# T tiles with 64 bytes more each, and the matrix of ones kept in the first stage's pool

## The chip, the cores and the metric

The kernel runs on one core of one Trainium2 chip. Its time is device time in microseconds (us). Five engines matter: TensorE (PE; its weight loads are PEld), VectorE (DVE), ScalarE (ACT), GpSimd (POOL), and SyncE (SP), which here issues every DMA.

## The reference

One encoder layer is applied to two batches, a prompt of 512 tokens and a sample of 1024, with the same weights and a model width of 1024. After an RMS norm, one input projection gives q, k, v and a gate for each of two attention branches, and two merge gates:

```python
    h = rmsnorm(x, norm_g)
    proj = h @ w_in
    qa, ka, va, za, qb, kb, vb, zb, ga, gb = jnp.split(proj, np.cumsum(SPLITS)[:-1], axis=-1)
    ...
    oa = neighbourhood_attention(qa, ka, va, rpb_a) * jax.nn.silu(za)
    oa = oa @ w_o_a
    ...
    ob = window_gqa_attention(qb, kb, vb, t5_table, sink_b) * jax.nn.silu(zb)
    ob = ob @ w_o_b
    merged = jax.nn.sigmoid(ga) * oa + jax.nn.sigmoid(gb) * ob
    return x + merged @ w_out
```

## The kernel before, in words

**Numbers.** Every float32 operand of a large product is split into two parts of type float32r: a high part (ACT copies it, L1104) and a low part (the source less the high part, DVE or POOL, L1109). A product is then three matmuls for each block of 128 rows, in `product`: high by high (L1221), high by low (L1222), low by high (L1223). The weights `whi`, `wlo` are loaded into the array, and 512 columns (256 in the very last product) of the other operand are moved through it. Sums over four or eight blocks stay in one of the PSUM banks p, s, o, t.

**Stages.** Norm of the prompt; attention of the prompt (projections L725, scores L919, softmax, transposes L968, products with v L1005); dense stage of the prompt (gates z, merge gates, branch projections, output projection); then attention and the dense stage of the sample. In `dense_phase` a pair of output blocks is either classic (eight blocks of h directly) or made with seven products in Strassen's way, for which sums of blocks of h are needed as moving operand. The prompt has only classic pairs (`CLASSIC_P`), the sample has three Strassen pairs of z, eight of the merge gates and three of the output projection (`CLASSIC_S`).

**The tiles called T.** Three kinds of operand share this name. (1) The sums of blocks of h for z and the merge gates of the sample: four sums, high and low, loaded from `t_d` by way of `U` and split in `stored_sums`. (2) The gated branches, split in `split_u`: four tiles for the prompt, in a pool of its own (`u_pool`); eight for the sample. (3) The sums of blocks of the merged activations, made on DVE in the tiles `S` and split in `sums`, ahead of the sample's output projection. A tile has 4 x 512 numbers per partition (8192 bytes), one slice of 512 for each block k. The eight tiles of the sample lie side by side in one pool and are used in turn by all three kinds. So the matmuls that read T are, for the prompt, 8 blocks x 2 branches x 4 k x 3 = 192; for the sample 384 with gated branches and 14 pairs x 4 products x 4 k x 3 = 672 with sums, 1056 in all.

**Where tiles lie.** The constants' pool (`cpool`) ends with a tile `left_pad` that serves only to fill it up; `right_pad` does so at the other end. Counted from the sizes in the order of allocation, T, whi, wlo, raw, S, U, C, the gates' `ot` and the sample's hh and hl all begin at a multiple of 512 bytes of their partition. The attention's tiles do not: pp (the transposed softmax, moving operand of L1005) begins 224 bytes past a multiple, hb (a gathered copy of h for branch B, loaded as weights in L725) 448 past.

**Order.** A planner (`Flow.run`) simulates the engines with fixed costs and writes out each engine's program: an operation starts when its inputs are ready and its tile's turn has come, lowest `prio` first, on the engine of its choice that ends first. It knows the number of buffers of a tile, not their size. DMAs are all issued on SP in the planned order. A tile allocated over older ones waits for their last readers.

**`ones`.** A matrix of 128 x 128 ones, set by DVE at the start (L404), is the stationary operand of a small matmul in `spread_rstd` (L453) that spreads a token's norm factor over the partitions.

Of the kernel before, what the change touches and what calls it, by code (L numbers as in the profile page):

```python
# [10 lines left out]
F32 = mybir.dt.float32  # L11
F32R = mybir.dt.float32r
# [13 lines left out]
CLASSIC_S = (1, 0, 1)  # L26
START = (-10, -6.5, -4, -3)
GATE = 2
FIRST_POOL = (0, 2)
NORM = (-20, -1, 0, 1)  # L30
P = 128
# [312 lines left out]
def encoder_kernel(  # L344
# [24 lines left out]
    dve = nc.vector  # L369
    pe = nc.tensor  # L370
# [29 lines left out]

    mhalf = cpool.tile([P, 8], F32, tag="mhalf", name="mhalf")
    dve.memset(mhalf, -0.5)
    ones = cpool.tile([P, P], F32, tag="ones", name="ones")
    dve.memset(ones, 1.0)  # L404
    gx = cpool.tile([P, KC], F32, tag="gx", name="gx")

    cpool.tile([P, 56], F32, tag="left_pad", name="left_pad")
# [8 lines left out]
    f = Flow(pspool)  # L416
# [27 lines left out]
    def spread_rstd(pool, r, t, rb, prio):  # L444

        diag = f.value(pool, [P, P], F32, "diag", 1)
        f.op(
            (("act", ACT_(P) + 40),), lambda e: act.activation(diag.t, ident, AF.Copy, scale=r.t),
            prio, new=[diag], use=[r],
        )  # L450
        ps = f.value(pspool, [P, 512], F32, "o", 2)
        f.op(
            (("pe", 215),), lambda e: pe.matmul(ps.t[:, :P], ones, diag.t, start=True, stop=True),  # L453
            prio, new=[ps], use=[diag],
        )
        f.op(
            (("act", ACT_(P, False)),),
            lambda e: act.activation(rb.t[:, t * P : (t + 1) * P], ps.t[:, :P], AF.Copy), prio, use=[ps],
            **({"into": [rb]} if t else {"new": [rb]}),
        )  # L460
# [609 lines left out]
    def dense_phase(geo, hh, hl, h_ops, o_stores, exps_done, start, opened, tp, up, p0, p1, p2, x_t, y_t, classic, after_gates=None, side=None):  # L1070
# [3 lines left out]
        nh = 512  # L1074
# [17 lines left out]

        dma = f.dma

        def tt(out, in0, in1, op, n, prio, psum=False, **kw):

            choice = (("dve", DVE_(n)),) if psum else any_tt(n)
            return f.op(choice, lambda e: engines[e].tensor_tensor(out(), in0(), in1(), op=op), prio, **kw)
# [16 lines left out]
        def moving_sums(tv, ops):  # L1115
            def mov(j):
                vh, vl = tv[j]
                return [(lambda k=k: vh.t[:, k], lambda k=k: vl.t[:, k], ops[j, k], [vh, vl]) for k in range(4)]

            return mov  # L1120

        def sums(prio, done):

            tv = [tuple(f.value(tp, [P, 4, sn], F32R, "T", 8) for _ in range(2)) for _ in range(4)]
            ops = {}
            for k in range(4):
                blk = lambda a, kk, n: (lambda: a.t[:, kk, n * sn : (n + 1) * sn].bitcast(F32))
                h = {(i, n, a): blk((hh, hl)[a], k + 4 * i, n) for i in range(2) for n in range(2) for a in range(2)}
                t = [tile_("S", 3) for _ in range(4)]

                def step(j, in0, block, part, op, new, other=None):
                    after = done[k + 4 * block[0], block[1]] if done else []
                    kw = {"new": [t[j]]} if new else {"into": [t[j]]}
                    use = [v for v in (other, None if new else t[j]) if v]
                    tt(
                        lambda v=t[j]: v.t[:, :sn], in0, h[*block, part], op, sn, prio, use=use, after=after, hold=[hh, hl], **kw
                    )


                for j, plus, minus in ((0, (0, 1), (0, 0)), (2, (1, 1), (0, 1))):  # L1140
                    after = done[k + 4 * plus[0], plus[1]] + done[k + 4 * minus[0], minus[1]] if done else []
                    tt(
                        lambda v=t[j]: v.t[:, :sn], h[*plus, 0], h[*minus, 0], ALU.subtract, sn, prio, new=[t[j]], after=after,
                        hold=[hh],
                    )
                    step(j, lambda v=t[j]: v.t[:, :sn], plus, 1, ALU.add, False)
                    step(j, lambda v=t[j]: v.t[:, :sn], minus, 1, ALU.subtract, False)
                after = done[k + 4, 1] if done else []
                tt(
                    lambda v=t[1]: v.t[:, :sn], h[1, 1, 0], lambda v=t[0]: v.t[:, :sn], ALU.subtract, sn, prio,  # L1150
                    new=[t[1]], use=[t[0]], after=after, hold=[hh],
                )
                step(1, lambda v=t[1]: v.t[:, :sn], (1, 1), 1, ALU.add, False)
                step(3, lambda v=t[1]: v.t[:, :sn], (1, 0), 0, ALU.subtract, True, t[1])
                step(3, lambda v=t[3]: v.t[:, :sn], (1, 0), 1, ALU.subtract, False)
                for j in (0, 2, 1, 3):
                    vh, vl = tv[j]
                    ops[j, k] = split(
                        lambda vh=vh, k=k: vh.t[:, k], lambda vl=vl, k=k: vl.t[:, k], lambda v=t[j]: v.t[:, :sn], sn, prio,
                        (vh, k == 0), (vl, k == 0), [t[j]],  # L1160
                    )

            return moving_sums(tv, ops)

        def stored_sums(prio):

            tv, ops = {}, {}
            for j in (1, 2, 0, 3):
                tv[j] = tuple(f.value(tp, [P, 4, nh], F32R, "T", 8) for _ in range(2))
                vh, vl = tv[j]  # L1170
                for k in range(4):
                    st = tile_("U", 4)
                    dma(
                        lambda st=st, j=j, k=k: nc.sync.dma_start(st.t, t_d[j, k]), 512 * nh, prio, new=[st],
                        after=[s[j] for s in t_stores],
                    )
                    ops[j, k] = split(
                        lambda vh=vh, k=k: vh.t[:, k], lambda vl=vl, k=k: vl.t[:, k], lambda st=st: st.t, nh, prio,
                        (vh, k == 0), (vl, k == 0), [st],
                    )  # L1180
            return moving_sums(tv, ops)
# [182 lines left out]
        def split_u(c, a, n, v, prio):  # L1364
            br, k = divmod(c, 4)
            key = br, a // nh
            new = key not in uv
            if new:
                uv[key] = tuple(f.value(up, [P, 4, nh], F32R, "T", 4 * len(halves)) for _ in range(2))
            vh, vl = uv[key]  # L1370
            cols = slice(a % nh, a % nh + n)
            u_ops.setdefault((*key, k), []).extend(split(
                lambda: vh.t[:, k, cols], lambda: vl.t[:, k, cols], lambda: v.t[:, :n], n, prio, (vh, new), (vl, new), [v],
            ))

        def with_x(c, a, n, v, prio):
# [64 lines left out]
        for m in range(8):  # L1441
# [5 lines left out]
            for n in halves:  # L1447
                gs_ = []
                for br in range(2):
                    ps = psum_(next(tags))  # L1450
                    vh, vl = uv[br, n]
                    movs = [
                        (lambda k=k, vh=vh: vh.t[:, k], lambda k=k, vl=vl: vl.t[:, k], u_ops[br, n, k], [vh, vl])
                        for k in range(4)
                    ]
                    product(ps, ws[br], movs, prio, True, True)
                    tag, bufs = (("C", n_c), ("ot", n_ot) if short else ("U", 4))[br]
                    g = tile_(tag, bufs)
                    dma(
                        lambda g=g, br=br, m=m, n=n: nc.sync.dma_start(g.t, g_d[br, m, :, half[n]]), 512 * nh,  # L1460
                        prio - 0.5, new=[g], after=stores["g", br, m, n],
                    )
                    tt(
                        lambda g=g: g.t, lambda ps=ps: ps.t, lambda g=g: g.t, ALU.mult, nh, prio, psum=True,
                        use=[ps, g], into=[g],
                    )
                    gs_.append(g)
                a, b = gs_
                tt(lambda a=a: a.t, lambda a=a: a.t, lambda b=b: b.t, ALU.add, nh, prio, use=gs_, into=[a])
                m_ops[m, n] = split(  # L1470
                    lambda m=m, n=n: hh.t[:, m, half[n]], lambda m=m, n=n: hl.t[:, m, half[n]], lambda a=a: a.t, nh,
                    prio, (hh, None), (hl, None), [a], after=h_reads,
                )
# [37 lines left out]

    f.stage(-1000, open=(r_h, d0["p"], rb_pool, early["p"], late["p"], norm_p), make=h_p)
    f.dma(lambda: nc.sync.dma_start(gx, norm_g), 4096, START[0] + 0.2, into=[gx_v])
    for t in range(gp.nb):
        h_ops["p"][t] = norm_tile(norm_p, x_p, *h_p, t, NORM[t], START[t], h_ops["p"][t - GATE][::2] if t >= GATE else ())
    setup(norm_p, gp.nb)
# [113 lines left out]
```

## Time and profile before

| what | value |
|---|---|
| median of three runs | 1195.18 us (1193.61 to 1196.21) |
| the profiled execution's own time | 1193.63 us |
| its span, first to last instruction | 1191.8 us |
| mean granted TensorE clock | 0.996 |
| PE, DVE, ACT, POOL busy, share of the span | 97%, 74%, 55%, 29% |
| HBM traffic | 137 GB/s over the span |

The span is that of one execution, and its times of day below count from its first instruction. A matmul's duration includes its passage through the array, and its end is modelled; the pace of a run of matmuls is read from starts. An engine's idle time is put down to what ended it.

### The profile page before, as it was taken

The page shows a single profiled execution, that of the slowest core. Times are in us where ns is not written, and L with a number is a line of the kernel's source. Part 1 is how long each engine was busy: PE and PEld are TensorE (multiplying, and loading weights), DVE is VectorE, ACT ScalarE, POOL GpSimd, SP SyncE. Part 2 cuts the span into 40 slices and gives each one's busy share as a digit, 9 for nine tenths or more (in the row PEclk, how much of TensorE's full clock was granted, in tenths as well). Part 3 has the DMA queues.
Part 4 walks back from the last instruction along what each step waited for, and adds up shares of the span by engine and source line. Part 5 has one row for each costly group of instructions (what it writes and reads, how often), then busy time and mean ns, then how long its engine had stood idle before and what let it go on. Part 6 is the DMA issues. An engine that isn't in the chain of part 4 may idle for free.

```text
span 1191.8 us, 18682 instructions
## 1 busy us (share of the span) xinstructions
PE 1156.6 (97%) x6118; PEld 981.4 (82%) x6118; DVE 878.8 (74%) x1977; ACT 660.0 (55%) x1504; POOL 342.5 (29%) x469
## 2 busy tenths in 40 slices
PE   7999899999999999999999989999999999999798
PEld 6889777888888898998997878878888888788687
DVE  6788888586655468878777888868976565497985
ACT  6967886453433346465669888866434344333330
POOL 4763654000011043343326454302311110131110
PEclk9999999999999999999999999999999999999999
DMA  9734223778875422120211122237773334573152
GB/s 302 258 110 137 80 65 106 215 237 259 261 212 180 152 74 63 26 66 22 78 50 50 34 63 45 45 103 265 198 220 133 104 118 156 191 246 107 46 176 97
DMA packets 124545, 159.35 MB, mean 134 GB/s; under 512 B 28272, under 2 KB 66928, under 8 KB 124448
## 3 DMA queue, kind: packets, MB, share of 16 engines
q1 hardware_dynamic: 124448, 158.16, 43.7%
q8 instruction: 48, 0.79, 0.3%
q14 instruction: 49, 0.40, 0.1%
HBM read 121.40 MB, written 41.44 MB: 137 GB/s over the span
## 4 chain that ended last, share of the span: by engine, by line
PE 83%; DVE 5%; POOL 3%; ACT 2%; issue 2%; DMA 1%; ACTq 0%; POOLq 0%; DVEq 0%
PE p L725 20%; PE s L919 5%; PE p L1221 5%; PE p L1223 5%; PE p L1222 4%; PE o L1005 4%; PE s L1221 4%; PE s L1222 4%; PE s L1223 4%; PE t L968 4%; PE o L1223 4%; PE o L1222 4%; PE o L1221 4%; PE t L1222 4%; PE t L1223 4%; PE t L1221 4%
## 5 line engine op out<-in xcount | busy, mean ns | idle before, releaser
L1104 ACT ACTIVATE whi<-raw 128x512 fp32r<-128x512 f32 (+1 forms) x160 | 92.5, 589 | 79.2 <-PE s L1222 18.0
L1109 POOL TENSOR_TENSOR wlo<-raw,whi 128x512 fp32r<-128x512 f32 (+1 forms) x34 | 46.3, 1361 | 310.7 <-ACT whi L1104 298.1
L725 PE MATMUL p<-wlo,hh 128*128 128x384 f32 x384 | 133.7, 348 | 0.0
L725 PE MATMUL p<-whi,hh 128*128 128x384 f32 x384 | 133.7, 348 | 0.0
L725 PE MATMUL p<-whi,hl 128*128 128x384 f32 x384 | 132.8, 346 | 0.0
L895 ACT ACTIVATE sb<-sb,mx 128x384 f32<-128x384 f32 (+1 forms) x192 | 108.9, 570 | 20.2 <-DVE mx L886 19.3
L1109 DVE TENSOR_TENSOR wlo<-raw,whi 128x512 fp32r<-128x512 f32 (+1 forms) x126 | 82.1, 662 | 38.9 <-ACT whi L1104 38.8
L725 PE MATMUL p<-whi,hb 128*128 128x384 f32 x384 | 108.8, 351 | 1.3 <-DVE qk L630 1.0
L979 DVE TENSOR_TENSOR pp<-t,pp 128x512 fp32r<-128x512 f32 (+1 forms) x136 | 84.8, 640 | 27.8 <-ACT pp L974 26.2
L974 ACT ACTIVATE pp<-t 128x512 fp32r<-128x512 f32 (+1 forms) x136 | 73.0, 558 | 46.2 <-PE t L968 45.8
L1005 PE MATMUL o<-pp,v 128*128 128x256 f32 (+1 forms) x368 | 81.9, 333 | 3.9 <-DVE pp L979 3.9
L950 POOL TENSOR_TENSOR sb<-sb,rs 128x384 f32<-128x384 f32 (+1 forms) x95 | 71.5, 770 | 45.6 <-DVE rs L944 40.1
L968 PE MATMUL t<-ident,sb 128*128 128x128 f32 x496 | 75.8, 277 | 7.4 <-DVE pp L979 4.9
L760 POOL TENSOR_TENSOR rs_r<-rs_v,mhalf 128x4 f32<-128x4 f32 (+1 forms) x72 | 80.3, 1115 | 5.4
L725 PEld LDWEIGHTS p<-whi,hh 128*128 128x128 f32 x384 | 72.6, 189 | 3.6 <-issue 2.9
L725 PEld LDWEIGHTS p<-whi,hb 128*128 128x128 f32 x384 | 69.7, 191 | 6.5 <-issue 2.2
L968 PEld LDWEIGHTS t<-ident,sb 128*128 128x128 f32 x496 | 57.9, 140 | 20.5 <-DVE pp L979 7.1
L725 PEld LDWEIGHTS p<-whi,hl 128*128 128x128 f32 x384 | 72.6, 189 | 1.9 <-issue 1.0
L725 PEld LDWEIGHTS p<-wlo,hh 128*128 128x128 f32 x384 | 72.6, 189 | 1.4 <-issue 1.0
L753 POOL TENSOR_SCALAR rs_v<-ss 128x4 f32<-128x4 f32 (+1 forms) x72 | 17.3, 241 | 183.2 <-DVE ss L746 178.7
L1005 PEld LDWEIGHTS o<-pp,v 128*128 128x128 f32 x368 | 58.2, 189 | 11.0 <-DVE pp L979 7.4
L725 PE MATMUL p<-wlo,hb 128*128 128x384 f32 x192 | 67.1, 350 | 0.0
(348 smaller groups left out, 3227.0 us busy)
## 6 DMA issues: line engine op xcount, KB each, us to landing
raw<-in_w_g_dram SPq DMA_DIRECT2D x96, 256.0 KB
w<-in_w_att_dram SPq DMA_DIRECT2D x48, 384.0 KB
g_d<-C SPq DMA_DIRECT2D x48, 256.0 KB
ot<-o_d SPq DMA_DIRECT2D x36, 256.0 KB
raw<-in_w_z_dram SPq DMA_DIRECT2D x32, 256.0 KB
raw<-in_w_out_dram SPq DMA_DIRECT2D x32, 256.0 KB
C<-g_d SPq DMA_DIRECT2D x24, 256.0 KB
out_dram<-C SPq DMA_DIRECT2D x23, 256.0 KB
```

The source lines that it names most:

```text
L725: pe.matmul(ps.t[:, :GW], part[u](k), mv.t[:, c], start=k == 0 and m == 0, stop=k == KC - 1 and m == 2,)
L760: lambda e: nc.gpsimd.tensor_tensor(r.t[:, :nn], rv.t[:, :nn], mhalf[:, :nn], op=ALU.pow),
L895: act.activation(sb.t[:, :width], sb.t[:, :width], AF.Exp, bias=mx.t[:, i : i + 1], scale=-1.0, accum_out=sm.t[:, i : i + 1],)
L968: pe.transpose(pt.t[:, u * P : (u + 1) * P], sbs[i].t[:, c * P : (c + 1) * P], ident)
L974: lambda e, pt=pt, pp=pp, nn=nn: act.activation(pp.t[:, 0, :nn], pt.t[:, :nn], AF.Copy),
L979: lambda e, pt=pt, pp=pp, nn=nn: dve.tensor_tensor(pp.t[:, 1, :nn], pt.t[:, :nn], pp.t[:, 0, :nn].bitcast(F32), op=ALU.subtract),
L1005: pe.matmul(out(), v.t[:, vs], mv(), start=first, stop=last)
L1104: (("act", ACT_(n)),), lambda e: act.activation(hi(), src(), AF.Copy), prio,
L1109: lambda e: engines[e].tensor_tensor(lo(), src(), hi().bitcast(F32), op=ALU.subtract), prio,
L1221: pe.matmul(out, hi.t[:, cs], mh(), start=first and k == 0, stop=False)
L1222: pe.matmul(out, hi.t[:, cs], ml(), start=False, stop=False)
L1223: pe.matmul(out, lo.t[:, cs], mh(), start=False, stop=last and k == len(ws) - 1)
```

## The change

Each T tile gets 16 numbers (64 bytes) more per partition, and is allocated as a flat row, of which `part(v, k, n)` cuts slice k. The eight tiles of the sample together take 512 bytes more. These come from `ones`, which leaves the constants' pool: it becomes a tile of the first norm stage's pool, set by an operation of the planner with the lowest `prio` of that stage.

```diff
+T_PAD = 16
...
-    ones = cpool.tile([P, P], F32, tag="ones", name="ones")
-    dve.memset(ones, 1.0)
...
-            (("pe", 215),), lambda e: pe.matmul(ps.t[:, :P], ones, diag.t, start=True, stop=True),
-            prio, new=[ps], use=[diag],
+            (("pe", 215),), lambda e: pe.matmul(ps.t[:, :P], ones.t, diag.t, start=True, stop=True),
+            prio, new=[ps], use=[diag, ones],
...
+        def part(v, k, n):
+
+            return v.t[:, k * n : k * n + n]
...
-                return [(lambda k=k: vh.t[:, k], lambda k=k: vl.t[:, k], ops[j, k], [vh, vl]) for k in range(4)]
+                return [(lambda k=k: part(vh, k, sn), lambda k=k: part(vl, k, sn), ops[j, k], [vh, vl]) for k in range(4)]
...
-            tv = [tuple(f.value(tp, [P, 4, sn], F32R, "T", 8) for _ in range(2)) for _ in range(4)]
+            tv = [tuple(f.value(tp, [P, 4 * sn + T_PAD], F32R, "T", 8) for _ in range(2)) for _ in range(4)]
...
-                tv[j] = tuple(f.value(tp, [P, 4, nh], F32R, "T", 8) for _ in range(2))
+                tv[j] = tuple(f.value(tp, [P, 4 * nh + T_PAD], F32R, "T", 8) for _ in range(2))
...
-                uv[key] = tuple(f.value(up, [P, 4, nh], F32R, "T", 4 * len(halves)) for _ in range(2))
+                uv[key] = tuple(f.value(up, [P, 4 * nh + T_PAD], F32R, "T", 4 * len(halves)) for _ in range(2))
...
+    ones = f.value(norm_p, [P, P], F32, "ones", 1)
+    f.op((("dve", 170),), lambda e: dve.memset(ones.t, 1.0), -30, new=[ones])
```

The other lines of the diff put `part(...)` in the place of `vh.t[:, k]` and `vl.t[:, k]` where these tiles are written and read.

## Rows read from the trace of the kernel before

**Rows 1.** The page: engines' busy time and share; the chain's shares.

```profile
PE 1156.6 (97%) x6118; PEld 981.4 (82%) x6118; DVE 878.8 (74%) x1977; ACT 660.0 (55%) x1504; POOL 342.5 (29%) x469
...
PE 83%; DVE 5%; POOL 3%; ACT 2%; issue 2%; DMA 1%; ACTq 0%; POOLq 0%; DVEq 0%
```

**Rows 2.** Windows: length, busy us of PE, PEld, DVE, ACT, POOL; PEclk, DMA.

```profile
230.00:325.00 95.00, 95.00 (x421) 78.74 (x420) 70.40 (x147) 44.58 (x79) 0.00 (x0) 1.00 0.83 247
...
850.00:1000.00 150.00, 150.00 (x664) 124.28 (x663) 99.39 (x154) 59.89 (x112) 26.20 (x18) 1.00 0.46 143
...
1100.00:1192.00 92.00, 81.67 (x361) 67.41 (x359) 71.73 (x114) 22.50 (x42) 12.91 (x9) 0.96 0.32 106
```

**Rows 3.** Instructions of line 1221: ns min/median/max, first and last start (us).

```profile
L1221 PE MATMUL p<-T,whi x104: 389/389/390, 333.9 to 1179.6; 128*128 128x512 f32 x104
```

**Rows 4.** Timeline of PE (start, us): first of twelve T matmuls; the thirteenth.

```profile
1174.81 0.39 PE L1221 MATMUL t<-T,whi 128*128 128x512 f32 x1
...
1177.53 0.39 PE L1221 MATMUL p<-T,whi 128*128 128x512 f32 x1
```

**Rows 5.** Timeline of PE: its longest wait, in brackets with what ended it.

```profile
1132.03 0.79 PE L1223 MATMUL p<-hh,wlo 128*128 128x512 f32 x1 [7.06 <-DVE wlo L1109]
1132.62 0.63 PE L1221 MATMUL p<-hh,whi 128*128 128x512 f32 x1
1133.04 0.63 PE L1222 MATMUL p<-hl,whi 128*128 128x512 f32 x1
```

**Rows 6.** The chain from 1096 to 1134 us, shares by line.

```profile
by line: DVE S L1098 48.0%; DVE T L1109 25.3%; DVE C L1098 8.2%; issue 5.5%; PE p L1223 3.2%; DVE U L1098 1.6%; DVE hl L1109 1.6%; PE s L1223 1.2%; PE s L1222 1.2%; PE s L1221 1.2%; PE p L1221 1.1%; PE p L1222 1.1%; DVE wlo L1109 1.0%; DVEq
```

**Rows 7.** Timeline of PE: pp matmuls, what follows; hh matmuls of 256 columns.

```profile
794.39 0.63 PE L1005 MATMUL o<-pp,v 128*128 128x512 f32 x2
794.86 0.39 PE L1221 MATMUL s<-hh,whi 128*128 128x512 f32 x1
...
477.98 0.87 PE L1005 MATMUL o<-pp,v 128*128 128x256 f32 x6
478.69 0.38 PE L822 MATMUL t<-ident,qk 128*128 128x128 f32 x2
...
1185.69 0.28 PE L1221 MATMUL t<-hh,whi 128*128 128x256 f32 x1
...
1187.13 0.28 PE L1221 MATMUL p<-hh,whi 128*128 128x256 f32 x1
```

**Rows 8.** Instructions of line 725 from 415 to 790 us, columns as rows 3.

```profile
L725 PE MATMUL p<-whi,hh x256: 331/336/451, 415.5 to 619.9; 128*128 128x384 f32 x128
...
L725 PE MATMUL p<-whi,hb x256: 331/337/670, 620.4 to 762.3; 128*128 128x384 f32 x128
```

**Rows 9.** Tile T on ACT: two kinds of writes; idle time before (us, times).

```profile
L1104 ACT ACTIVATE T<-U x16: 618/633/635, 803.0 to 823.6; 128x512 fp32r<-128x512 f32 x16
...
L1104 ACT ACTIVATE T<-C x8: 621/633/635, 226.5 to 257.2; 128x512 fp32r<-128x512 f32 x8
...
  DMA U<-t_d: 5.6, 4
```

**Rows 10.** Tile T on DVE: writes of the last kind; idle time before all.

```profile
L1109 DVE TENSOR_TENSOR T<-S,T x14: 684/694/1779, 1098.0 to 1126.7; 128x512 fp32r<-128x512 f32 x14
...
  ACT T L1104: 16.4, 16
```

**Rows 11.** Tile pp: the low half's writes on DVE, columns as rows 3.

```profile
L979 DVE TENSOR_TENSOR pp<-t,pp x136: 407/691/697, 43.4 to 792.9; 128x512 fp32r<-128x512 f32 x112, 128x256 fp32r<-128x256 f32 x24
```

**Rows 12.** Tile T from 200 to 420 us: its first readers.

```profile
L1221 PE MATMUL o<-T,whi x16: 389/389/390, 328.5 to 363.1; 128*128 128x512 f32 x16
```

**Rows 13.** Timeline of the first 8 us: ones, its first reader, DVE's next work.

```profile
0.85 0.17 DVE L404 MEMSET ones<- 128x128 f32 x1
...
7.00 0.80 PE L453 MATMUL o<-diag,ones 128*128 128x128 f32 x2 [0.52 <-ACT diag L448]
7.82 1.29 DVE L570 TENSOR_TENSOR wlo<-w,whi 128x768 fp32r<-128x768 f32 x1 [6.81 <-ACT whi L565]
```

More of the change, by code (lines that the diff above doesn't have):

```diff
@@ L1158, in sums @@
                     ops[j, k] = split(
-                        lambda vh=vh, k=k: vh.t[:, k], lambda vl=vl, k=k: vl.t[:, k], lambda v=t[j]: v.t[:, :sn], sn, prio,
+                        lambda vh=vh, k=k: part(vh, k, sn), lambda vl=vl, k=k: part(vl, k, sn), lambda v=t[j]: v.t[:, :sn], sn, prio,
                         (vh, k == 0), (vl, k == 0), [t[j]],
@@ L1177, in stored_sums @@
                     ops[j, k] = split(
-                        lambda vh=vh, k=k: vh.t[:, k], lambda vl=vl, k=k: vl.t[:, k], lambda st=st: st.t, nh, prio,
+                        lambda vh=vh, k=k: part(vh, k, sn), lambda vl=vl, k=k: part(vl, k, sn), lambda st=st: st.t, nh, prio,
                         (vh, k == 0), (vl, k == 0), [st],
@@ L1372, in split_u @@
             u_ops.setdefault((*key, k), []).extend(split(
-                lambda: vh.t[:, k, cols], lambda: vl.t[:, k, cols], lambda: v.t[:, :n], n, prio, (vh, new), (vl, new), [v],
+                lambda: part(vh, k, nh)[:, cols], lambda: part(vl, k, nh)[:, cols], lambda: v.t[:, :n], n, prio, (vh, new), (vl, new), [v],
             ))
@@ L1452, in dense_phase @@
                     movs = [
-                        (lambda k=k, vh=vh: vh.t[:, k], lambda k=k, vl=vl: vl.t[:, k], u_ops[br, n, k], [vh, vl])
+                        (lambda k=k, vh=vh: part(vh, k, nh), lambda k=k, vl=vl: part(vl, k, nh), u_ops[br, n, k], [vh, vl])
                         for k in range(4)
```

## The prediction

> **What bounds the kernel now.** I began with the page: PE is busy for 1156.6 us, 97% of the span, and the chain that ended last lies on it for 83% [rows 1]. Whatever the change does must therefore show as PE's pace between matmuls or as a gap in PE. The windows by stage say where gaps are [rows 2]: in the prompt's dense stage (230 to 325 us here) and the sample's (850 to 1000) PE is busy for all of the window, at a granted clock of 1.00. Only the last window, 1100 to 1192, has room: 81.67 busy of 92.00, clock 0.96.
>
> Next, the matmuls that read T. They form twelve groups of 104 (four banks by three lines), 1248 in all, of which one stands in [rows 3]. A duration has a modelled end, so I trust starts: from 1174.81 to 1177.53 us lie twelve T matmuls, 2.72 us, or **226.7 ns each** [rows 4]. That stretch had no wait, and 226.7 ns at 2.4 GHz is 544 cycles for 512 columns.
>
> Last, the one gap in the dense stages: before 1132.03 PE stood 7.06 us for wlo from DVE, and the next matmuls start 0.42 us apart instead of 0.227, so TensorE had fallen to its lower level, 1.2 GHz, after that idle time [rows 5]. The chain there is DVE's: S sums 48.0% and T writes 25.3% of 1096 to 1134 us [rows 6]. It is the one place where a slower or faster write to T would move the end.
>
> **The change, part by part.** No instruction is removed or added. What alters is where T tiles lie, and where `ones` lies and when it is set.
>
> *Matmuls that read T.* Today every T tile, and whi and wlo beside it, begins at a multiple of 512 bytes. After the change the sample's eight tiles begin 0, 64, ... 448 past one, the prompt's four 256 to 448 past one. A T tile's four slices are 2048 bytes apart, so all share the tile's place. Off the old place are all 192 matmuls of the prompt and 7/8 of the sample's 1056, that is 924: 1116 in all. No row shows T anywhere else, so I bound its price by the moving operand that does begin elsewhere, pp, 224 bytes past a multiple. With 512 columns two pp matmuls take 794.39 to 794.86 us, 235 ns each, 8.3 above T's pace [rows 7]: 1116 x 8.3 ns = 9.3 us slower. With 256 columns six take 477.98 to 478.69, 118.3 ns each, against 120.0 for hh at a multiple of 512, twelve from 1185.69 to 1187.13 [rows 7]: 1.7 ns less, 1.9 us faster over 1116, or 3.8 us if it grows with the columns. The ends differ in sign, and both matmuls also differ from T's in stationary operand and neighbours. The nearest pair that differs in place and little else is L725 with hh (at a multiple) and hb (448 past one) as stationary operand: 336 and 337 ns [rows 8]. I take **0**, and keep -3.8 and +9.3 us as ends.
>
> By the Trainium skill (SBUF — State Buffer, section "Who interferes with whom") PE and ACT never wait for another engine at SBUF; the only contention is at the port pair that VectorE and GpSimd share. By that rule this term is 0; by the 235 ns row alone it would be +9.3 us.
>
> *ACT's writes to T.* 56 (16 each of three kinds, 8 of the prompt), median 633 ns, shortest 618 [rows 9]. If place explained the spread, 56 x 15 ns = 0.8 us of ACT's time is to be had; upward I allow the same. ACT is busy for 22.50 of the last 92 us [rows 2], so the other engines' work covers it. Where ACT does lead, DVE waited for its T write 16 times [rows 10]: at most 16 x 15 ns = 0.2 us. I take 0.
>
> *Writes to the low half.* 54 on DVE and 2 on POOL. For T<-S on DVE the shortest is 684 ns and the median 694 [rows 10]; the same operation to pp, 224 bytes off, has a median of 691 over both its forms [rows 11]. The 14 of T<-S stand in the chain of [rows 6] or just before it: 14 x 10 ns = 0.14 us either way. I take 0. One of the 14 lasted 1779 ns, 1.1 us over the median, with its ACT input long written; a meeting with POOL is likely, and the order of instructions on both engines stays as it is.
>
> *Tiles over older tiles.* T's tiles lie over tiles of an earlier stage, and each grows by 64 bytes, so a first write may get another old reader to wait for. Prompt: T is written from 226.5 to 257.2 us and first read at 328.5 [rows 9, 12], about 70 us of cover. Sample: the attention stage's last pp matmuls start at 794.39 [rows 7], T's first write at 803.0, and the writes there already waited on the load U<-t_d, 5.6 us in all [rows 9]. Cost 0. If that cover were gone, such a wait would hold ACT, with `whi` splits queued behind, and PE at the sample's first read of T; a wait as long as the present ones, 5.6/4 = 1.4 us, is the upper end.
>
> *The memset of `ones`.* 0.17 us on DVE at 0.85 us, read by PE first at 7.00; DVE's next work starts at 7.82, after 6.81 us without any [rows 13]. It becomes the first operation of the written order; PE's matmul keeps waiting for it, with ACT's diag last. What queues behind it on DVE is that work at 7.82. Cost 0; 0.17 us if the cover were gone. The tile leaves its 512 bytes of the constants to T's padding, so the tiles between move by just 512 bytes. No DMA moves in SP's queue or POOL's instructions in theirs: T is never the target of a DMA.
>
> **Sum:** five terms of 0 against the profiled execution's own 1193.63 us (1.8 us more than its span). The median of the three runs is 1195.18, 1.55 above it; I forecast on the median: **1195.2 us**.
>
> **Rivals.** *Slower: place costs the moving operand.* Begun off a multiple of 512, T is read as pp is, at 235 ns a matmul. For it: the 512-column pp row of [rows 7], with no wait before it. Against: [rows 8] and the 256-column rows. It starts to decide at 2.2 ns per matmul (2.4 us / 1116). Full price 1195.2 + 9.3 = 1204.5 us; chance 0.12.
>
> *Faster: today's common place is what costs.* T, whi and wlo all begin at the same place, and 544 cycles for 512 columns leaves 32 over. If some of those come from two reads that meet, spreading T frees them: up to 3.8 us by [rows 7], 1191.4 us. For it: 118.3 against 120.0 ns. Against: the excess is the same 32 cycles at 256 columns (120.0 ns is 288 cycles), as for a fixed step between matmuls. Chance 0.13.
>
> *The stall of [rows 5] changes length.* DVE reaches it after a full row of sums; one meeting of a POOL and a DVE instruction more or less, like the 1779 ns write, is worth about 1.1 us of either sign: 1194.1 or 1196.3 us. It stays within what a measurement can tell, so it belongs to the forecast's case.
>
> *It doesn't do what it says.* hh, hl, whi, wlo, S, C and raw stay at multiples of 512, and one T tile of the sample's eight too. If it is their meeting that counts, nothing moves: the forecast again.
>
> **How the numbers follow.** A measurement of this kernel tells apart about 0.2%, 2.4 us (the three runs span 2.6). The likeliest case, in which nothing moves or less than that, has 0.75; the faster rival 0.13; the slower 0.12. Those are the three chances. The likeliest case holds 1192.8 to 1197.6; from there I reach down to 1191.4, the faster rival's full price, and up to 1199.5, about half of the slower one's, which leaves out less than 2 in 10.
>
> **What would show it.** Right: twelve T matmuls still in 2.72 us, T writes still at medians of 633 and 694 ns, and a gap near 7 us in the first Strassen pair of the output projection. Wrong: a pace of T matmuls that differs from that of the hh matmuls beside them (slower near 0.235 us, faster below 0.226), or a gap of PE before a first read of T. If the time moved while that pace stayed, the gap before 1132 or a changed order would be the cause, and the place of T innocent.

## The result and the profile after

The changed kernel takes 1199.24 us (median of 6 runs, 1197.28 to 1201.01). The kernel before, run six times as well, takes 1193.73 (1192.38 to 1196.21). The ratio is **1.0042, with a 95% interval of 1.0029 to 1.0056**: slower by 0.42%, which is 3.5 to 6.7 us. The profiled execution of the changed kernel is its own fastest run, 1197.28 us, so its span stands only 3.7 us above the span of before.

The lines from 700 on are shifted: the three matmuls of `product` are now L1224 to L1226 (before: L1221 to L1223), the split is L1107 and L1112, the sums are L1101. The page, with the span and the busy times; it answers to [rows 1]:

```profile
span 1195.5 us, 18684 instructions
...
PE 1160.9 (97%) x6118; PEld 980.4 (82%) x6118; DVE 877.7 (73%) x1977; ACT 660.2 (55%) x1504; POOL 342.7 (29%) x469
```

The instructions are the same in number on every engine. PE is busy for 4.3 us more; the other engines moved by 1.1 us or less, in both directions. So the time went into PE, and not into a gap. The windows by stage, columns as in [rows 2]; the first line is the kernel before, for a window that [rows 2] does not have, the others are the changed kernel:

```profile
325.00:400.00 75.00, 75.00 (x333) 62.16 (x332) 36.89 (x59) 23.03 (x37) 9.07 (x7) 1.00 0.62 190
...
230.00:325.00 95.00, 95.00 (x421) 78.68 (x420) 71.66 (x151) 44.72 (x80) 0.00 (x0) 1.00 0.80 247
325.00:400.00 75.00, 75.00 (x329) 61.46 (x328) 37.16 (x58) 23.50 (x38) 9.07 (x7) 1.00 0.62 196
850.00:1000.00 150.00, 150.00 (x656) 122.94 (x655) 98.17 (x153) 59.85 (x111) 26.86 (x17) 1.00 0.46 142
```

The count of matmuls is what to read here, because a PE that is "busy for all of the window" hides its pace. From 230 to 325 us no matmul reads T, and 421 begin, as before. Where T is read, 329 begin instead of 333 (325 to 400 us) and 656 instead of 664 (850 to 1000). The granted clock is 1.00 in all three windows, as it was, so TensorE ran at 2.4 GHz and the lost matmuls are not the clock's.

The same can be seen within one stretch of the timeline of PE (start, duration in us): the first row begins twelve matmuls that read T, the second twelve and the third 24 that read hh and hl, the fourth twelve that read T again; the last two rows stand at either end of twelve with 256 columns.

```profile
1167.30 0.40 PE L1224 MATMUL t<-T,whi 128*128 128x512 f32 x1
...
1170.08 0.40 PE L1224 MATMUL p<-hh,whi 128*128 128x512 f32 x1
...
1172.81 0.39 PE L1224 MATMUL s<-hh,whi 128*128 128x512 f32 x1
...
1178.25 0.40 PE L1224 MATMUL t<-T,whi 128*128 128x512 f32 x1
...
1181.04 0.40 PE L1224 MATMUL p<-T,whi 128*128 128x512 f32 x1
...
1189.33 0.28 PE L1224 MATMUL t<-hh,whi 128*128 128x256 f32 x1
...
1190.76 0.28 PE L1224 MATMUL p<-hh,whi 128*128 128x256 f32 x1
```

Twelve T matmuls take 2.78 us (231.7 ns each) and 2.79 us (232.5), where they took 2.72 in [rows 4]. Twenty-four hh and hl matmuls from 1172.81 take 5.44 us, 226.7 ns each: the old pace. The four T products from 1178.25 to 1189.33, 48 matmuls, take 11.08 us (230.8 ns each); before they went from 1174.81 to 1185.69, 10.88 us. The twelve matmuls of 256 columns take 1.43 us, against 1.44 in [rows 7].

Averaged over the kernel, from one start to the next (intervals with no wait before the second, 1242 of them before and 1244 after), a T matmul went from 226.7 to 231.3 ns. That is 1248 x 4.6 ns = 5.7 us. The hh and hl matmuls of 512 columns went from 227.0 to 227.2, 1422 x 0.2 = 0.3 us. Together 6.0 us, inside the interval of 3.5 to 6.7: the whole loss is there.

The line that answers to [rows 3], columns as there; its median rose from 389 to 396 ns:

```profile
L1224 PE MATMUL p<-T,whi x104: 388/396/404, 335.5 to 1183.1; 128*128 128x512 f32 x104
```

The other terms. T's writes on ACT and on DVE, columns as in [rows 9, 10]:

```profile
L1107 ACT ACTIVATE T<-U x16: 619/632/633, 802.7 to 823.2; 128x512 fp32r<-128x512 f32 x16
...
L1112 DVE TENSOR_TENSOR T<-S,T x14: 680/682/1789, 1101.9 to 1130.5; 128x512 fp32r<-128x512 f32 x14
```

The longest wait of PE, in the timeline of PE; it answers to [rows 5]:

```profile
1135.81 0.79 PE L1226 MATMUL p<-hh,wlo 128*128 128x512 f32 x1 [6.85 <-DVE wlo L1112]
```

ACT's medians stay at 632 to 633 ns, DVE's T<-S falls by 12 ns (14 writes, 0.2 us in all), one of them still lasts over 1.7 us, and the stall is 0.21 us shorter.

### The profile page after: what moved, and what is told of

The parts are those of the page before. It is cut to its first block, busy times and chain, and to the rows that moved or that the text cites. A ratio compares the mean times of both kernels' runs of the same rounds, so it can differ in the third digit from the quotient of the medians.

```text
span 1195.5 us, 18684 instructions
## 1 busy us (share of the span) xinstructions
PE 1160.9 (97%) x6118; PEld 980.4 (82%) x6118; DVE 877.7 (73%) x1977; ACT 660.2 (55%) x1504; POOL 342.7 (29%) x469
## 4 chain that ended last, share of the span: by engine, by line
PE 83%; DVE 5%; POOL 3%; ACT 2%; issue 2%; DMA 1%; SPq 0%; POOLq 0%; ACTq 0%; DVEq 0%
PE p L724 19%; PE s L918 5%; PE p L1224 5%; PE p L1226 5%; PE p L1225 5%; PE s L1224 4%; PE s L1225 4%; PE s L1226 4%; PE o L1004 4%; PE t L967 4%; PE o L1224 4%; PE o L1225 4%; PE o L1226 4%; PE t L1225 4%; PE t L1224 4%; PE t L1226 4%
## 5 line engine op out<-in xcount | busy, mean ns | idle before, releaser
L1107 ACT ACTIVATE whi<-raw 128x512 fp32r<-128x512 f32 (+1 forms) x160 | 92.6, 589 | 85.0 <-PE s L1225 18.3
L1112 POOL TENSOR_TENSOR wlo<-raw,whi 128x512 fp32r<-128x512 f32 (+1 forms) x34 | 46.7, 1374 | 317.3 <-ACT whi L1107 170.8
L1112 DVE TENSOR_TENSOR wlo<-raw,whi 128x512 fp32r<-128x512 f32 (+1 forms) x126 | 81.3, 656 | 38.8 <-ACT whi L1107 38.7
L759 POOL TENSOR_TENSOR rs_r<-rs_v,mhalf 128x4 f32<-128x4 f32 (+1 forms) x72 | 80.3, 1116 | 5.4
```

The source lines that it names most:

```text
L759: lambda e: nc.gpsimd.tensor_tensor(r.t[:, :nn], rv.t[:, :nn], mhalf[:, :nn], op=ALU.pow),
L1107: (("act", ACT_(n)),), lambda e: act.activation(hi(), src(), AF.Copy), prio,
L1112: lambda e: engines[e].tensor_tensor(lo(), src(), hi().bitcast(F32), op=ALU.subtract), prio,
```

## The experiments

The result left three questions: is it the place of T at all, or the moved `ones`; what place relative to what; and is there a better one than today's. All eight kernels below start from the changed kernel with its padding set to 0. Filler tiles, which nothing reads or writes, stand before (`T_LEAD`) and behind (`T_TAIL`) the sample's eight T tiles, in numbers of 4 bytes, so that everything else stays where it is. The prompt's tiles get spare room (`P_PAD`), and each tile's slices begin `P_OFF` numbers into it: a pair for each branch, high part and low part, in the runs that have two numbers a branch. The instructions and their order on each engine are the same in all of them. "Place" is the start in the partition modulo 512 bytes; whi and wlo lie at 0 unless said.

```diff
+        if name == "t_s" and T_LEAD:
+            self.pool.tile([P, T_LEAD], F32, tag="t_lead", name="t_lead", bufs=1)
...
-                uv[key] = tuple(f.value(up, [P, 4 * nh + T_PAD], F32R, "T", 4 * len(halves)) for _ in range(2))
+                uv[key] = tuple(f.value(up, [P, 4 * nh + (P_PAD if short else T_PAD)], F32R, "T", 4 * len(halves)) for _ in range(2))
+                if short:
+                    uv[key][0].off, uv[key][1].off = P_OFF[br]
```

**No spread, all else as changed.**

```diff
-T_PAD = 16
+T_PAD = 0
+T_LEAD, T_TAIL = 0, 128
```

> The changed kernel with the 64 bytes taken back: ones stays in the first stage's pool, every T tile is 8192 bytes and begins at a multiple of 512 again, 512 unused bytes lie behind the sample's T tiles. If the place of T is the cause (theory: place), T matmuls are back at 226.7 ns and the time is that of the kernel before, 1193 to 1195 us, ratio 1.000 +- 0.0015. If moving ones, or the 512 bytes by which the tiles of the left side moved, is the cause (rival: layout), the time stays near 1199 us, ratio 1.004.

Measured: 1193.18 us, ratio 0.9992 [0.9981, 1.0003]. Timeline of PE, the first of the last 48 T matmuls and the matmul behind them:

```profile
1173.52 0.39 PE L1233 MATMUL t<-T,whi 128*128 128x512 f32 x1
...
1184.40 0.28 PE L1233 MATMUL t<-hh,whi 128*128 128x256 f32 x1
```

10.88 us for 48, the pace of before. `ones` is still where the change put it and the helper `part` still cuts the slices, so neither costs anything that can be told: the place of T is what cost.

**All T of the sample at one place, 64.** The alternative to "another place costs" is "the high and the low part at different places cost". Here the sample's tiles all lie at 64; in the prompt, branch 0 has both parts at 64, and branch 1 has 0 and 64.

```diff
+T_LEAD, T_TAIL = 16, 112
+P_PAD = 128
+P_OFF = ((16, 16), (0, 16))
```

> As the one without padding, but all eight T tiles of the sample begin at the same place, 64 bytes past a multiple of 512. In the prompt, branch 0 has its high and low tile both 64 past, branch 1 has them at 0 and 64. Theory absolute place (a moving operand off a multiple of 512 is slow by itself): the sample's T matmuls run at about 232 ns, 1056 x 5 ns = 5 us, ratio about 1.004; in the prompt branch 0 is at 232, branch 1 between. Rival difference (it costs when one moving operand and the next lie at different places): the sample's T matmuls stay at 226.7 ns, ratio 1.000, prompt branch 0 at 226.7, branch 1 at 230 to 233.

Measured: 1198.34 us, ratio 1.0025 [1.0012, 1.0038].

```profile
1182.25 0.40 PE L1233 MATMUL t<-T,whi 128*128 128x512 f32 x1
...
1193.25 0.28 PE L1233 MATMUL t<-hh,whi 128*128 128x256 f32 x1
```

11.00 us for 48, 229.2 ns each, with both parts at the same place. In the prompt the mean is 229.8 with 64 and 64, and 230.8 with 0 and 64. So a common place is no cure: 64 itself costs 2.5 ns a matmul. And a high part at 0 does not run at the old pace when its low part lies elsewhere.

**All T of the sample at 256.** In the prompt: branch 0 at 32 and 32, branch 1 at 0 and 256.

```diff
+T_LEAD, T_TAIL = 64, 64
+P_PAD = 128
+P_OFF = ((8, 8), (0, 64))
```

> As the last, but all eight T tiles of the sample begin 256 bytes past a multiple of 512; in the prompt branch 0 has both tiles 32 bytes past one, branch 1 has them at 0 and 256. Absolute place modulo 512: about 232 ns in the sample, ratio about 1.004. Absolute place modulo 256 (or less): 226.7 ns in the sample and in branch 1, ratio 1.000, and branch 0 slow. Difference: the sample and branch 0 at 226.7 ns, branch 1 slow.

Measured: 1195.53 us, ratio 1.0014 [1.0002, 1.0026]. The timeline of PE holds the prompt's first product of branch 0 (o), the one of branch 1 that follows (t) with its last rows, and the sample's last 48:

```profile
330.33 0.40 PE L1233 MATMUL o<-T,whi 128*128 128x512 f32 x1
...
333.13 0.40 PE L1233 MATMUL t<-T,whi 128*128 128x512 f32 x1
...
334.98 0.39 PE L1235 MATMUL t<-T,wlo 128*128 128x512 f32 x1
335.21 0.39 PE L1233 MATMUL t<-T,whi 128*128 128x512 f32 x1
335.43 0.39 PE L1234 MATMUL t<-T,whi 128*128 128x512 f32 x1
335.66 0.39 PE L1235 MATMUL t<-T,wlo 128*128 128x512 f32 x1
335.89 0.40 PE L1233 MATMUL p<-T,whi 128*128 128x512 f32 x1
...
1176.99 0.39 PE L1233 MATMUL t<-T,whi 128*128 128x512 f32 x1
...
1187.87 0.28 PE L1233 MATMUL t<-hh,whi 128*128 128x256 f32 x1
```

The sample at 256 runs at 10.88 us for 48, the pace of place 0: **what counts is the place modulo 256 bytes, not 512** (that it is not modulo 128 is shown by the run with T at 128, below). At 32 twelve matmuls take 2.80 us, 233.3 ns each. The product at 0 and 256 that follows takes 2.76, but not evenly: its first eight need 1.85 us (231 ns each), its last four 0.91 (227.5). A disturbed stretch has an after-effect, here of some eight matmuls. Its length differs: in the sample, after a product on T at 128 (the run below) the hh and hl matmuls are back at 227.4 ns or less from the fourth on, and after T at 64 only from the eleventh. It fits this that in the changed kernel no product on T ran below a mean of 228.8 ns, those with a tile at place 0 or 256 included.

**The weights moved as well.** `left_pad` gets 64 bytes more, so whi, wlo and the sample's T, hh and hl all lie at 64; the prompt's hh and hl stay at 0; the prompt's T lie at 0 (branch 0) and 64 (branch 1).

```diff
+T_LEAD, T_TAIL = 0, 112
+P_PAD = 128
+P_OFF = ((0, 0), (16, 16))
+LEFT_MORE = 16
...
-    cpool.tile([P, 56], F32, tag="left_pad", name="left_pad")
+    cpool.tile([P, 56 + LEFT_MORE], F32, tag="left_pad", name="left_pad")
```

> As the one without padding, but everything on the left side of the memory lies 64 bytes further: whi, wlo, the sample's hh and hl and T all begin 64 past a multiple of 512, tiles of the right side stay. In the prompt hh is at 0, T of branch 0 at 0 and 0, of branch 1 at 64 and 64. Theory relative place (the moving operand must lie at the place of the weights): the sample's dense matmuls stay at 226.7 ns, the prompt's hh matmuls and branch 0 are slow, branch 1 fast. Theory absolute place: all dense matmuls of the sample, T and hh, go to about 232 ns, so (1056 + about 1100) x 5 ns = 11 us there, ratio about 1.009, while the prompt's hh matmuls and branch 0 stay at 226.7. The attention's tiles also move by 64 bytes, so its stage may change by itself; the pace by stage decides, not the sum.

Measured: 1201.59 us, ratio 1.0055 [1.0037, 1.0073]. Timeline of PE: 24 matmuls of the prompt on hh and hl, then T of branch 0 (o), then T of branch 1 (t), and the sample's last 48:

```profile
322.26 0.39 PE L1233 MATMUL p<-hh,whi 128*128 128x512 f32 x1
...
327.86 0.39 PE L1233 MATMUL s<-hh,whi 128*128 128x512 f32 x1
...
333.46 0.40 PE L1233 MATMUL o<-T,whi 128*128 128x512 f32 x1
...
336.26 0.39 PE L1233 MATMUL t<-T,whi 128*128 128x512 f32 x1
...
339.00 0.39 PE L1233 MATMUL p<-T,whi 128*128 128x512 f32 x1
...
1180.93 0.39 PE L1233 MATMUL t<-T,whi 128*128 128x512 f32 x1
...
1191.81 0.28 PE L1233 MATMUL t<-hh,whi 128*128 128x256 f32 x1
```

The same stage in the windows view:

```profile
230.00:325.00 95.00, 95.00 (x409) 76.23 (x408) 70.88 (x149) 43.33 (x77) 0.00 (x0) 1.00 0.80 245
```

With everything at 64 the sample keeps its old pace, 10.88 us for 48. In the prompt hh at 0, a multiple of 512, now needs 5.60 us for 24, 233.3 ns each, and the stage without any T begins 409 matmuls instead of 421. So does T at 0 (2.80 us for twelve), while T at 64, after it, needs 2.74. Neither 0 nor 64 is good or bad by itself: **the pace depends on where the moving operand lies against where the weights lie**. This is the run that ends the theory of absolute places. It also speaks against another engine as the cause: the prompt's hh and hl matmuls take a mean of 233.3 ns where DVE is busy for the whole interval (327 of them) and 233.3 where it is idle throughout (169), and the same where ACT is busy or idle.

**Other distances.** The sample's T lies at 128, and the four slices of the prompt's tiles at places of their own, in steps of 16 bytes and more (`P_OFF` has four numbers a branch in this run and the next, one for each slice, high and low part alike).

```diff
+T_LEAD, T_TAIL = 32, 96
+P_PAD = 256
+P_OFF = ((0, 4, 8, 12), (16, 24, 32, 40))
```

> T of the sample all 128 bytes past a multiple of 512, and in the prompt eight places at once, high and low tile alike: branch 0 has its slices k = 0 to 3 at 0, 16, 32, 48 bytes past a multiple of 256, branch 1 at 64, 96, 128, 160. whi and wlo stay at a multiple of 512. Theory relative place modulo 256: 226.7 ns only at 0, 229 to 234 ns at the others and at 128 in the sample; the worst at 32 or below, as 32 gave 233.6. Rival, a bank of 64 bytes: 16, 32 and 48 like 0 at 226.7 to 228, the others slow. If some place is better than 0, it shows below 226 ns.

Measured: 1202.43 us in its one run, against a median of 1194.40 before.

```profile
1183.31 0.40 PE L1241 MATMUL t<-T,whi 128*128 128x512 f32 x1
...
1194.51 0.28 PE L1241 MATMUL t<-hh,whi 128*128 128x256 f32 x1
```

A distance of 128 takes 11.20 us for 48, 233.3 ns each. The prompt's part of the run says little of single places: the slices are disturbed by their neighbours (229.6 ns at place 0). But all eight products of branch 1 repeat the same twelve intervals to the nanosecond (230, 226, 234, 234, 231, 238, 232, 230, 232, 235, 228, 231), also the first, beside which DVE starts 0.17 us later than beside the others and POOL does nothing. That speaks for PE's own sequence as the cause. No steady stretch ran below 226 ns.

**Only the low weights moved.** wlo lies at 64 (`WLO_MORE` unused numbers stand before its first buffer), everything else that the sample's dense stage reads at 0. Theories: a matmul pays for the distance to its own weights, or to those that are loaded for the next matmul while it runs. In each group of three, the third reads wlo; the second has wlo as its next.

```diff
+T_LEAD, T_TAIL = 0, 0
+P_PAD = 256
+P_OFF = ((48, 56, 60, 62), (64, 1, 2, 20))
+WLO_MORE = 16
...
+                        if v.tag == "wlo" and WLO_MORE and not self.filled:
+                            self.filled = v.args[0].tile([P, WLO_MORE], F32, tag="w_fill", name="w_fill", bufs=1)
```

> T, hh and whi of the sample at multiples of 512 as before, only wlo begins 64 bytes past one. A product's matmuls are high by high, high by low (both with whi as weights) and low by high (wlo). Theory, the weights that are loaded for the next matmul while this one moves its operand: the second of each three is slow (about 233 ns, as with weights at 64 and the moving operand at 0), the first and the third stay at 226.7; about 900 x 6.5 ns = 5.9 us, ratio 1.004 to 1.005. Rival, a matmul's own weights: the third is slow, the second not; same sum. Rival, only T matters: nothing moves. In the attention's projections wlo is the moving operand and hh the weights: there the matmul that moves wlo should be slow by 6 ns, 576 in all, partly covered by waits. The eight places in the prompt are 192, 224, 240, 248 (branch 0) and 256, 4, 8, 80 bytes (branch 1) past a multiple of 256: 226.7 for 256 in its first matmul, 229 to 234 for the others, 4 and 8 bytes slow as well if the place counts to the byte.

Measured: 1205.39 us, ratio 1.0095 [1.0077, 1.0112], the slowest of all. Timeline of PE, six T matmuls and the seventh's start:

```profile
1186.07 0.39 PE L1241 MATMUL t<-T,whi 128*128 128x512 f32 x1
1186.30 0.39 PE L1242 MATMUL t<-T,whi 128*128 128x512 f32 x1
1186.53 0.40 PE L1243 MATMUL t<-T,wlo 128*128 128x512 f32 x1
1186.76 0.39 PE L1241 MATMUL t<-T,whi 128*128 128x512 f32 x1
1186.99 0.39 PE L1242 MATMUL t<-T,whi 128*128 128x512 f32 x1
1187.22 0.40 PE L1243 MATMUL t<-T,wlo 128*128 128x512 f32 x1
1187.45 0.39 PE L1241 MATMUL t<-T,whi 128*128 128x512 f32 x1
```

Six take 1.38 us, 230 ns each. Over all threes of the sample the means are 228.4 and 229.2 ns for the two with whi and 235.7 for the one with wlo; on hh and hl they are 228.4, 229.2 and 235.7. My theory of the next weights had the second as the slow one, and half the loss: it fell. The matmul's own weights are the better reading, but not the whole, since the two others, with weights and moving operand both at 0, lost 2 to 3 ns as well. Nor do the three run alike when they share one distance: with T at 64 they take 229.5, 227.8 and 230.1 ns. The slow matmul with wlo takes 235.4 ns where DVE is busy for the whole interval and 235.3 where it is idle, which speaks for PE with itself and against a meeting with another engine. Where in PE's path it arises stays open. The expectation for the attention missed: the 384-column matmuls that move wlo did not become 6 ns slower, their median interval is 174 ns before and 175 here.

**The attention's tiles put at multiples of 256.** If the distance costs there too, kt, q, hb, pp and others that lie off could be made faster. `FILL` puts that many unused numbers before the first buffer of a tile.

```diff
+LEFT_MORE = -32
+FILL = {"qk": 16, "pp": 56}
...
+    cpool.tile([P, 32], F32, tag="first_pad", name="first_pad")
```

> No padding of T (as the first experiment), and the attention's operands put at multiples of 256 bytes too: the identity matrix (was 128 past), qk, kt, q, hb, mask, bias, sb (were 192 past one of 256) and pp (was 224 past). Theory relative place modulo 256: the products with v of 512 columns go from 229 to 235 ns to 226.7, 128 x 5 ns = 0.6 us at the most, projections with hb stay near 173.3 ns; as PE waits for other engines in much of this stage, the time is 0 to 1 us less than before, ratio 0.999 to 1.000. Rival, the place counts for more in transposes and scores as well: more than 2 us less, ratio below 0.998.

Measured: 1193.12 us, ratio 0.9994 [0.9983, 1.0005]; no difference that can be told. Timeline of PE, pp with 512 columns, two matmuls and what follows:

```profile
793.12 0.61 PE L1018 MATMUL o<-pp,v 128*128 128x512 f32 x2
793.57 0.39 PE L1239 MATMUL s<-hh,whi 128*128 128x512 f32 x1
```

Here the two take 0.45 us, against 0.47 in [rows 7]; but over all pp matmuls of 512 columns (start to start without a wait, 85 and 86 intervals) the mean is 231.8 ns in both kernels. They come in runs of two to four, shorter than the after-effect seen at 32 bytes, so a steady pace can't be read from them; whether that is why no effect of place shows is open.

**wlo moved by 256.** If the rule is a distance modulo 256, wlo at 256 must be free, and the prompt's high and low parts 256 apart as well (`P_OFF` now has four numbers for each part of each branch).

```diff
+P_PAD = 256
+P_OFF = (((0,) * 4, (64,) * 4), ((64,) * 4, (0,) * 4))
+WLO_MORE = 64
```

> T, hh and whi of the sample at multiples of 512, wlo 256 bytes past one; in the prompt the high tile of one branch and the low tile of the other lie 256 bytes past one too, so that successive matmuls read at two places 256 apart, and so do the weights. Theory relative place modulo 256: everything stays at 226.7 ns and the time is that of the kernel before, ratio 0.999 to 1.001. Rival modulo 512: the matmuls around each load of wlo are slow as with wlo at 64, about 13 ns for each three, 900 x 13 = 12 us, ratio 1.010.

Measured: 1193.75 us, ratio 1.0003 [0.9988, 1.0017].

```profile
1173.89 0.39 PE L1241 MATMUL t<-T,whi 128*128 128x512 f32 x1
...
1184.77 0.28 PE L1241 MATMUL t<-hh,whi 128*128 128x256 f32 x1
```

10.88 us for 48, the old pace, with whi at 0, wlo at 256 and T at 0. The prompt's T products, with high and low parts 256 apart, run at 226.7 ns too.

**All of them against the pace alone.** Mean from one start to the next of 512-column matmuls, without a wait before the second and below 270 ns; the loss is 1248 times the first difference and 1422 times the second, to 226.7 and 227.0 of before. The last column is the ratio less 1, times the time before, with its interval; for the 128 row it is the one run less the median before.

| kernel | T, ns | hh and hl, ns | loss by the pace, us | measured, us |
|---|---|---|---|---|
| changed kernel | 231.3 | 227.2 | 6.0 | 5.0 (3.5 to 6.7) |
| no spread | 226.8 | 227.0 | 0.1 | -1.0 (-2.3 to 0.4) |
| T at 64 | 229.3 | 227.5 | 4.0 | 3.0 (1.4 to 4.5) |
| T at 256 | 227.5 | 227.0 | 1.0 | 1.7 (0.2 to 3.1) |
| weights at 64 | 227.4 | 230.4 | 5.7 | 6.6 (4.4 to 8.7) |
| T at 128 | 232.8 | 227.2 | 7.9 | 8.0 |
| wlo at 64 | 231.3 | 231.1 | 11.6 | 11.3 (9.2 to 13.4) |
| attention's tiles | 226.8 | 226.9 | 0.0 | -0.7 (-2.0 to 0.6) |
| wlo at 256 | 226.8 | 227.0 | 0.1 | 0.4 (-1.4 to 2.0) |

Each loss by the pace lies within its interval where there is one, from -1 to +11 us; the 128 row is a single run. No kernel is faster than the one before by more than the measurement can tell.

## Why the prediction was right or wrong

The time, 1199.24 us, lies just within the range of 1191.4 to 1199.5, but not where the forecast of 1195.2 put it, and the case that came true is the one given 0.12. That the range holds it is luck: its upper end was set at about half of the slower rival's price to leave out little chance, not by a price, and the loss came out at about half, 5.0 us against 9.3.

*What bounds the kernel* held. The change had to show as PE's pace or as a gap in PE, and it shows as pace, in windows where PE counts as busy throughout both times. The sign to watch that the prediction named, the pace of T matmuls against the hh matmuls beside them, is what decided: 231.3 and 227.2 ns.

*Matmuls that read T* is the step that failed: "I take **0**". The measured term is 5.7 us. The choice rested on L725 with hh and hb as "the nearest pair that differs in place and little else" [rows 8]. It was nearest in place and far in shape: 384 columns instead of 512. (Its 336 and 337 ns are also durations, which the prediction had set aside in favour of starts.) The run with wlo at 64 shows that shape directly, for there wlo is L725's moving operand at a new place: the mean start interval of all 384-column projections is 185.2 ns before and 185.1 there, waits in part included, and the median 174 and 175. The run that put hb at a multiple of 256 shows the other side: the median of the matmuls on hb went from 174 to 175 ns. So at 384 columns place moves the pace by about 1 ns and not by 6, and the row could not have shown the price. The 256-column rows spoke against a loss in the same way; with wlo at 64 the 256-column matmuls even went from 119.7 to 117.7 ns, so there the sign is the other one.

*The upper end*, 9.3 us from pp at 235 ns, had the right sign by luck. With pp and v at multiples of 256 the mean over all pp matmuls is still 231.8 ns, so place was not shown to be what that row measured. (That mean, 5.1 ns above T's pace, times 1116 would have given 5.7 us, the measured term, by chance.) The price per matmul (8.3 ns there, 4.6 in the mean here, 6.6 at a steady distance of 32 or 128) was too high; the count, 1116, was too low, since the tiles at 0 and 256 pay too, by the after-effect.

*The rule of the Trainium skill* (SBUF — State Buffer, section "Who interferes with whom"), that PE never waits for another engine at SBUF, would make this term 0, and the term is 5.7 us. What the runs show does not look like another engine's doing, by the fixed patterns and the equal paces with DVE busy and idle, so they do not contradict the rule in what it says of other engines; it does not reach this case, and the measurement decides.

*The slower rival* was right in its mechanism, place costs the moving operand, and in the point from which it decides, 2.2 ns a matmul. Its condition was wrong: not "off a multiple of 512", but away from the weights' place modulo 256.

*The faster rival*, that the common place of T, whi and wlo is what costs, is the reverse of what holds at 512 columns. There the common place is what keeps the excess at 544 - 512 = 32 cycles; at a distance of 32, 128 or 192 the 233.3 ns are 560 cycles at 2.4 GHz, 16 more. At 256 columns, from which the rival took its case, the one run that shows it has the rival's sign (119.7 to 117.7 ns).

*ACT's writes, the low half's writes, tiles over older tiles, the memset:* each 0 in the sum, and nothing in the runs asks for more: medians of 632 to 633 ns, 12 ns less on 14 writes (0.2 us), and the kernel without the spread, which keeps the moved `ones`, at 0.9992 of before. *The stall* changed by 0.21 us, far less than the 1.1 us allowed for.

## What to carry to other kernels

Where dense float32r matmuls run back to back at 512 columns, let the moving operand and the weights begin at the same place modulo 256 bytes; spreading either over other places cost up to 1% of the time here and gained nothing. A place is good or bad only against another tile's place, so a filler tile in front of one pool can slow a stage whose own tiles have not moved. When PE reads as busy throughout, count the matmuls of a window or take the starts of twelve: the durations in the timeline, rounded to 10 ns, moved from 0.39 to 0.40 us, and their ends are modelled.

## What was not expected of the hardware

- The pace of 512-column matmuls depends on the distance of the moving operand from the weights, modulo 256 bytes: 226.7 ns at 0, 229.2 at 64, 233.3 at 32, at 128 and at 192 (hh at 0 with weights at 64). At 384 columns it moved by about 1 ns, and at 256 columns it became faster by 2 ns in the one run that shows it.
- The pace has a memory: after a product at 32, one at 0 and 256 needs some eight matmuls to fall from 231 to 227.5 ns. After T at 128 it is three matmuls, after T at 64 ten.
- One of the two weight tiles 64 bytes off slows all three matmuls of a group, to 228.4, 229.2 and 235.7 ns. That is 13.2 ns over three times 226.7. One matmul of the three lies at a distance of 192, whose steady price is 6.6 ns, so the three lose twice as much as that one alone would. By what path stays open, as do distances of a few bytes, which were tried only mixed.
